# Layer 0's later modulation chunks as single VectorE steps, token-major products of 512 columns: a two-layer trunk on one Trainium2 core

## The chip, the cores and the metric

The kernel runs on one core of one Trainium2 chip. The metric is the time of an execution on the device in microseconds (us). The engines are named as in the profile: PE is TensorE (matmul), DVE is VectorE, ACT is ScalarE, POOL is GpSimd, SP is SyncE, which here issues the loads of the weights.

## What is computed

A trunk of two layers over 256 tokens of 1024 features (`x`) and 256 tokens of context (`xc`), which only the first layer updates.

```python
def layer_forward(x, xc, mod, mod_c, lp, update_ctx):
    sh1, sc1, g1, sh2, sc2, g2 = jnp.split(mod, N_MOD, axis=-1)      # 6 x 1024
    ...
    h = modulate(rmsnorm(x, lp['norm1_g']), sh1, sc1)
    p = h @ lp['w_in']                  # u, v, q, k, va, hyena, gates
    ...
    x = x + g1 * merge_branches(p, attn, lp)
    h = modulate(rmsnorm(x, lp['norm2_g']), sh2, sc2)
    x = x + g2 * conv_ffn(h, lp)
    # the same for xc, if update_ctx

def merge_branches(p, attn, lp):
    a = spatial_gating_mixer(...); hy = hyena_mixer(...)
    g_a, g_b, g_c = jnp.split(jax.nn.sigmoid(p[..., OFF_GATE:]), N_BRANCH, axis=-1)
    m = g_a * (a @ wb[0]) + g_b * (attn @ wb[1]) + g_c * (hy @ wb[2])
    return m @ lp['w_out']

    # for each layer i:
    mod = (jax.nn.silu(c) @ ada_w[i] + ada_b[i])[:, None, :]
    mod_c = (jax.nn.silu(c_ctx) @ ada_w[i] + ada_b[i])[None, None, :]
```

The modulation `mod` is thus a product of a vector (two vectors in layer 0, `c` and `c_ctx`) with a matrix of 1024 x 6144. Its first third (`sh1`, `sc1`) is needed at the layer's start, `g1` after the output projection, the rest in the feed-forward.

## The kernel before, in words

Activations lie feature-major: 128 features on the partitions, the tokens as columns, 512 in layer 0 (x and context) and 256 in layer 1. A dimension of 1024 is 8 tiles (`k`). Every product is done as three fp32r matmuls on parts split into high and low: `wh·rl`, `wh·rh`, `wl·rh` (`mm_k`, L308 to L310). The weights are loaded by SP into four slots of 128 x 2048 (`wraw`), their high part is cast by ACT (L248) and their low part subtracted by DVE (L255), both `AHEAD` parts before PE needs them; four parts are two pieces of 24 matmuls.

The work is a list `items` that `run_items` goes through: dense items (a chunk of weights and what to do with it), native items (a raw tile of weights that is used unsplit, loaded one ahead by `load_native`) and calls. Beside it runs `side`, a queue of generators (the filter of the hyena branch, the spatial gate, hyena, attention): `pump` lets them go on by a step at each evacuation in `fm_run`. A layer's items are in order: u and v; 6 hyena chunks; 4 chunks of q and k, 2 of va; 12 gate chunks, between them, two places later (`LEAD`), 12 branch products; the output projection; the feed-forward with 11 pairs of up-projections, in which the next layer's modulation is worked out too.

The products v and va are token-major (`tm_use`): the tokens are the stationary side, the weights the moving one, 256 columns at a time, in two chunks.

The modulation of layer 0: its first third comes at the start. Chunks 1 and 2 (features of index f = 16 to 47, in tiles of 128) are 16 native items `ada`, one behind each of the 6 hyena chunks, the 4 of q and k, the 2 of va and the first 4 gates. Each is 8 fp32 matmuls of 32 columns on four column tiles of PE (L379) and a `pump`; the eighth of a chunk is followed by a transpose on DVE (L422). Layer 1's modulation goes another way (`ada_f`, L401): a step on DVE multiplies a row of 128 x 1024 weights with `scb`, the SiLU of the vector spread over the partitions, and sums it into one column of `mod`; `spread_c` makes `scb` before the first of them.

What the names in the rows are: `hd`, `tot`, `nsum` and `Fe`/`Fo` belong to the hyena filter (`filters`), `P`, `yT`, `Zo` to the hyena convolution, `pc` to the short convolution behind the hyena chunks, `S`, `P__n` and `PT` to attention.

Of the kernel before, what the change touches and what calls it, by code (L numbers as in the profile page):

```python
# [19 lines left out]
D = 1024  # L20
KD = 8
# [73 lines left out]
def trunk_kernel(ctx: ExitStack, tc: tile.TileContext, A: dict, out: bass.AP):  # L95
# [110 lines left out]
    def cuts(kind, kt, ncols):  # L206


        if kind == "m":
            return [[(k, min(k + 4, kt), c, c + 128) for k in range(0, kt, 4)] for c in range(0, ncols, 128)]  # L210
        return [[(k, k + 2, 0, ncols) for k in range(0, kt, 2)]]

# [6 lines left out]
    def run_items():  # L219
# [49 lines left out]

        ctl.update(due=0, at=0, ahead=AHEAD[0], load=load_to, prime=prime)  # L270
        pos = 0
# [46 lines left out]
    def fm_run(tiles, R, s0, s1, mid=None):  # L318

        n = len(R[0])  # L320
        ps = [psm.tile([128, 512], F32, tag="m", name="mm") for _ in tiles]
        for k in range(n):
            mm_k([p[:, 0:s1 - s0] for p in ps], [W for W, _, _ in tiles], R, k, s0, s1, n)
        if mid:
            mid()
        for (_, evac, m), p in zip(tiles, ps):
            evacuate(evac(m, p, s0, s1))
            ctl["due"] += ctl["pace"][(s1 - s0) // 256 - 1 if n > 4 else 3]
            pump(int(ctl["due"]))
            ctl["due"] %= 1  # L330

    def fm_chunk(R, segs, evac, nm=2):
# [36 lines left out]

    def ada(l, ch, k):  # L370
        src = A["ada_w"][l, k * 128:(k + 1) * 128, ch * 2048:(ch + 1) * 2048]

        def use(w):
            if k == 0:
                ada.ps = psm.tile([128, 512], F32, tag="m", name="ada")
            ps = ada.ps
            v = w.rearrange("p (t j i) -> p j t i", j=4, i=32)
            for j in range(4):
                mm(ps[32 * j:32 * j + 32, :], lhsT=scc[:, k, :], rhs=v[:, j], start=(k == 0), stop=(k == KD - 1),  # L379
                   tile_position=(0, 32 * j))  # L380
            if k == KD - 1:
                ada_evac(l, ch, ps)
            pump()
        native(src, use)

    def spread_c():

        for m in range(2):
            act(out=scb[m], in_=scb[m], func=AF.Silu)  # L389

    def ada_f(l, ch, k, rows):


        def use(w):
            if ch == k == 0:
                spread_c()
            junk = U("junk", BF16, 1024)
            for t in range(2):
                for m in range(rows):
                    f = ch * 16 + 2 * k + t  # L400
                    vec.scalar_tensor_tensor(out=junk, in0=w[:, t * 1024:(t + 1) * 1024], scalar=1.0, in1=scb[m],  # L401
                                             op0=ALU.mult, op1=ALU.mult, accum_out=mod[l][:, f, m:m + 1])
            if k == KD - 1:
                t0 = ch * 16
                b = prm[:, P_AB + 48 * l + t0:P_AB + 48 * l + t0 + 16].unsqueeze(2).to_broadcast([128, 16, rows])
                o = mod[l][:, t0:t0 + 16, 0:rows]
                vec.tensor_tensor(out=o, in0=o, in1=b, op=ALU.add)
                gains(l, ch, rows)
        native(A["ada_t"][l - 1, ch * KD + k], use)

    def gains(l, ch, rows):

        if ch != 1:
# [3 lines left out]
            vec.scalar_tensor_tensor(out=gs[l][:, w_, :, 0:rows], in0=sc, scalar=1.0, in1=g, op0=ALU.add, op1=ALU.mult)  # L417

    def ada_evac(l, ch, ps):

        tr = U("adat")
        vec.transpose(out=tr, in_=ps)  # L422
        t0 = ch * 16
        b = prm[:, P_AB + 48 * l + t0:P_AB + 48 * l + t0 + 16].unsqueeze(2).to_broadcast([128, 16, 2])
        vec.tensor_tensor(out=mod[l][:, t0:t0 + 16, :], in0=tr.rearrange("p (t i) -> p t i", i=32)[:, :, 0:2], in1=b,
                          op=ALU.add)
        gains(l, ch, 2)

# [440 lines left out]
    def layer(l):  # L869
# [62 lines left out]

        def tm_use(c, ntt, dst, func, period=None):

            def use(piece):
                W = piece(0)
                rh, rl = S["H"]
                for t in range(ntt):
                    ps = psm.tile([128, 512], F32, tag="m", name="mt")
                    o = ps[:, 0:256]  # L940
                    for k in range(KD):
                        wh, wl = W[k]
                        x, y = rh[k][:, t * 128:(t + 1) * 128], rl[k][:, t * 128:(t + 1) * 128]
                        mm(o, lhsT=x, rhs=wl, start=(k == 0), stop=False)  # L944
                        mm(o, lhsT=x, rhs=wh, start=False, stop=False)  # L945
                        mm(o, lhsT=y, rhs=wh, start=False, stop=(k == KD - 1))  # L946
                    act(out=S[dst][t][:, c * 256:(c + 1) * 256], in_=o, func=func)  # L947
                    if (t + 1) % (period or ctl["pace"][2]) == 0:
                        pump()
            return use  # L950

        for c in range(2):
            dense(col(512 + c * 256), KD, 256, tm_use(c, 2 * nseg, "v", AF.Gelu, 1), "t")

        def go_sgu():
            S["sgu"] = start(sgu(l, nseg, S["u"], S["v"]))
            if l == 0:
                start(filters([iter(())], [(0, 1)]))
            S["part"] = []
        call(go_sgu)  # L960
# [24 lines left out]

        ada_todo = [(l, ch, k) for ch in (1, 2) for k in range(KD)] if l == 0 else []

        def hy_chunks():
            for c in range(6):
                dense(col(2560 + c * 256), KD, 256, late(lambda c=c: fm_chunk(S["H"], full, hy_evac(c))))  # L990
                if ada_todo:
                    ada(*ada_todo.pop(0))

            def go():
                S["hy"] = start(hyena(l, nseg, S["part"]))
            call(go)
# [8 lines left out]
        def qkv_chunks():  # L1005
            def alloc():
                S["qk"] = {(s, m): U("qk") for s in range(2) for m in range(4)}
                S["va"] = [U("va") for _ in range(4)]
            call(alloc, False)
            for i, c0, segs in ((0, 1024, full), (1, 1536, [(0, 512)])):  # L1010
                for c in range(2):
                    dense(col(c0 + c * 256), KD, 256,
                          late(lambda c=c, i=i, sg=segs: fm_chunk(S["H"], sg, qk_evac(i, c))))
                    if ada_todo:
                        ada(*ada_todo.pop(0))
# [6 lines left out]
            for c in range(2):  # L1022
                dense(col(2048 + c * 256), KD, 256, tm_use(c, 4, "va", AF.Copy), "t")
                if ada_todo:
                    ada(*ada_todo.pop(0))

# [44 lines left out]
        todo = [(b, j) for b in ORDER for j in range(4)]  # L1071
        for i in range(len(todo) + LEAD):
            if i >= LEAD and todo[i - LEAD][1] == 0:
                call(br_split(todo[i - LEAD][0]), False)
            if i < len(todo):
                b, j = todo[i]
                dense(col(4096 + b * 1024 + j * 256), KD, 256, late(lambda b=b, j=j: fm_chunk(S["H"], full, gate_evac(b, j))))
                if ada_todo:
                    ada(*ada_todo.pop(0))
            if i >= LEAD:  # L1080
# [3 lines left out]
                def before(b=b, j=j):  # L1084
                    if b == ORDER[-1]:
                        if j == 0:
                            S["M"] = [[], []]
                        for i in range(2):
                            S["M"][i] += fm("Mh" if i == 0 else "Ml", 2, T, F32R)
                call(before, False)  # L1090
                dense(wb[:, :, j * 256:(j + 1) * 256], 4, 256, late(lambda b=b, j=j: fm_chunk(S["B"], full, br_evac(b, j))))

# [5 lines left out]
        def res_evac(gate_t, j, nm, last):  # L1098
# [110 lines left out]

        for j in range(11):  # L1210
            up_pair(j)
            if j >= AJ:
# [139 lines left out]
    def finish():  # L1352
        rb = rbc.pop(0)
        for k in range(KD):
# [17 lines left out]

_NAMES = ["xT", "prm", "kst", "dec", "ada_w", "ada_0", "ada_t", "cc", "w_in", "sgu_w", "sgu_norm_g", "sgu_b", "rpb", "hy_filt_w3", "hy_skip",
          "w_branch", "w_out", "ffn_w_up", "ffn_w_down"]


def layout(i):
# [21 lines left out]
    for l in range(DEPTH):  # L1399
# [7 lines left out]
    r["ada_0"] = i["ada_w"][0, :, 0:2048].reshape(8, 128, 2, 4, 256).transpose(3, 0, 1, 2, 4).reshape(4, 8, 128, 512)  # L1407
    r["ada_w"] = i["ada_w"][0:1]

    r["ada_t"] = i["ada_w"][1:].transpose(0, 2, 1).reshape(DEPTH - 1, 24, 2, 128, D).transpose(0, 1, 3, 2, 4).reshape(  # L1410
        DEPTH - 1, 24, 128, 2 * D)
    r["cc"] = np.stack([i["c"][0], i["c_ctx"]])
# [36 lines left out]
```

## Time and profile before

| | us |
|---|---|
| median of 3 runs | 1455.67 (1454.6 to 1455.97) |
| the profiled execution | 1453.75 |
| its span in the profile | 1451.7 |
| PE busy | 1412.6 (97%) |
| DVE busy | 1006.3 (69%) |
| ACT busy | 666.9 (46%) |
| POOL busy | 89.2 (6%) |

The granted clock of PE is 0.995 on average. A matmul's duration overlaps with the next one's, so what a matmul costs is read from the distance of two starts, not from its duration. The span is what the profiler saw between first and last instruction, and the rows' times count from its start.

### The profile page before, as it was taken

What the parts mean: (1) busy time and instruction counts of PE and PEld (TensorE: products, weight loads), DVE (VectorE), ACT (ScalarE), POOL (GpSimd) and SP (SyncE); (2) the same over time, 40 slices, a digit from 0 to 9 for tenths busy, and PEclk for the clock granted to TensorE, in tenths of its full rate; (3) what the DMA queues carried; (4) which work ended last, traced back from release to release, by engine and by line L of the source; (5) the groups of instructions that cost most, each with busy time, mean ns of one, the idle gap of its engine ahead of it and who ended that gap; (6) DMA issues with size and microseconds to landing.
All of it is one profiled execution on the core that took longest, in us unless ns stands there. A gap on an engine that the chain in (4) does not pass through costs nothing.

```text
span 1451.7 us, 22050 instructions
## 1 busy us (share of the span) xinstructions
PE 1412.6 (97%) x8724; PEld 1215.9 (84%) x8724; DVE 1006.3 (69%) x1870; ACT 666.9 (46%) x1368; POOL 89.2 (6%) x96
## 2 busy tenths in 40 slices
PE   6999999999999999999999999999999999999997
PEld 4887777767787889988878778999789899999997
DVE  5666744676775567666887997578767787776575
ACT  4542332434664335533322433465336755665352
POOL 0020201110000000000001220000110000000000
PEclk9999999999999999999999999999999999999998
DMA  9835434233222523244488455545233445556542
GB/s 350 270 130 189 145 129 162 102 115 124 80 88 76 171 97 108 74 159 145 155 265 263 143 174 156 163 142 171 88 117 123 142 158 192 171 175 172 199 143 68
DMA packets 190594, 221.21 MB, mean 152 GB/s; under 512 B 5563, under 2 KB 174556, under 8 KB 185372
## 3 DMA queue, kind: packets, MB, share of 16 engines
q1 hardware_dynamic: 184848, 206.06, 43.0%
q0 software_dynamic: 3344, 10.75, 2.5%
q10 hardware_dynamic: 2300, 3.01, 0.7%
q8 instruction: 68, 1.11, 0.3%
q14 instruction: 34, 0.28, 0.1%
HBM read 216.65 MB, written 1.05 MB: 150 GB/s over the span
## 4 chain that ended last, share of the span: by engine, by line
PE 82%; DVE 9%; DMA 3%; ACT 3%; issue 1%; ACTq 0%; POOL 0%; SPq 0%; DVEq 0%; POOLq 0%
PE mm L308 22%; PE mm L310 22%; PE mm L309 22%; DMA w<-w_in 2%; DVE wp L255 2%; PE mt L944 1%; PE mt L945 1%; PE mt L946 1%; PE pv L813 1%; PE PT L800 1%; DMA aw<-ada 1%; PE S L776 1%; PE ada L379 1%; ACT wp L248 1%; PE Ze L634 1%
## 5 line engine op out<-in xcount | busy, mean ns | idle before, releaser
L308 PE MATMUL mm<-hl,wp 128*128 128x256 f32 (+1 forms) x1476 | 500.5, 339 | 0.8 <-DVE hl L479 0.7
L310 PE MATMUL mm<-hh,wp 128*128 128x256 f32 (+1 forms) x1476 | 491.5, 333 | 0.5 <-DVE wp L255 0.5
L309 PE MATMUL mm<-hh,wp 128*128 128x256 f32 (+1 forms) x1476 | 491.2, 333 | 0.0
L255 DVE TENSOR_TENSOR wp<-w,wp 128x512 fp32r<-128x512 f32 (+1 forms) x576 | 375.3, 695 | 24.3 <-ACT wp L248 21.2
L248 ACT CAST wp<-w 128x512 fp32r<-128x512 f32 (+1 forms) x576 | 321.4, 610 | 94.9 <-DMA w<-ffn_w_down 45.7
L308 PEld LDWEIGHTS mm<-hl,wp 128*128 128x128 f32 x1476 | 280.3, 190 | 37.4 <-issue 6.4
L309 PEld LDWEIGHTS mm<-hh,wp 128*128 128x128 f32 x1476 | 280.4, 190 | 29.4 <-issue 3.1
L310 PEld LDWEIGHTS mm<-hh,wp 128*128 128x128 f32 x1476 | 280.2, 190 | 28.4 <-DVE wp L255 0.7
L308 PE MATMUL mm<-ml,wp 128*128 128x256 f32 (+1 forms) x392 | 125.9, 321 | 0.0
L310 PE MATMUL mm<-mh,wp 128*128 128x256 f32 (+1 forms) x392 | 125.4, 320 | 0.0
L309 PE MATMUL mm<-mh,wp 128*128 128x256 f32 (+1 forms) x392 | 125.3, 320 | 0.0
L401 DVE SCALAR_TENSOR_TENSOR junk<-wn,scb 128x1024 bf16<-128x1024 f32 x64 | 79.2, 1238 | 2.8 <-ACT scb L389 1.4
L308 PEld LDWEIGHTS mm<-ml,wp 128*128 128x128 f32 x392 | 74.7, 190 | 6.0 <-issue 0.8
L309 PEld LDWEIGHTS mm<-mh,wp 128*128 128x128 f32 x392 | 74.7, 190 | 5.4
L310 PEld LDWEIGHTS mm<-mh,wp 128*128 128x128 f32 x392 | 74.7, 190 | 5.4
L1103 DVE SCALAR_TENSOR_TENSOR xT<-mm,mod,xT 128x256 f32<-128x256 f32 x72 | 33.7, 481 | 62.7 <-PE mm L310 61.1
L1137 ACT ACTIVATE a<-mm,prm 128x256 f32<-128x256 f32 (+1 forms) x48 | 30.8, 644 | 88.1 <-PE mm L310 87.0
L944 PE MATMUL mt<-wp,hh 128*128 128x256 f32 x224 | 64.3, 287 | 2.0 <-ACT va L947 1.3
L308 PE MATMUL mm<-bl,wp 128*128 128x512 f32 (+1 forms) x192 | 65.4, 341 | 0.0
L981 DVE SCALAR_TENSOR_TENSOR a<-mm,prm,a 128x255 f32<-128x255 f32 (+1 forms) x48 | 27.9, 582 | 53.2 <-ACT a L1137 53.2
L310 PE MATMUL mm<-bh,wp 128*128 128x512 f32 (+1 forms) x192 | 64.6, 336 | 0.0
L309 PE MATMUL mm<-bh,wp 128*128 128x512 f32 (+1 forms) x192 | 64.6, 336 | 0.0
(623 smaller groups left out, 2041.0 us busy)
## 6 DMA issues: line engine op xcount, KB each, us to landing
w<-w_in SPq DMA_DIRECT2D x56, 1024.0 KB, 5.2
w<-ffn_w_up SPq DMA_DIRECT2D x44, 1024.0 KB, 5.0
wn<-ada_t SPq DMA_DIRECT2D x24, 1024.0 KB, 5.0
wn<-ada_w SPq DMA_DIRECT2D x16, 1024.0 KB, 4.8
w<-w_branch SPq DMA_DIRECT2D x24, 512.0 KB, 3.4
w<-ffn_w_down SPq DMA_DIRECT2D x16, 768.0 KB, 5.1
w<-ffn_w_down SPq DMA_DIRECT2D x16, 640.0 KB, 4.5
aw<-ada SPq DMA_DIRECT2D x32, 256.0 KB, 5.4
```

The source lines that it names most:

```text
L248: nc.scalar.copy(h, src)
L255: vec.tensor_tensor(out=l_, in0=src, in1=spl[st["lo"]][0], op=ALU.subtract)
L308: mm(o, lhsT=wh, rhs=rl, start=(k == 0), stop=False)
L309: mm(o, lhsT=wh, rhs=rh, start=False, stop=False)
L310: mm(o, lhsT=wl, rhs=rh, start=False, stop=(k == n - 1))
L379: mm(ps[32 * j:32 * j + 32, :], lhsT=scc[:, k, :], rhs=v[:, j], start=(k == 0), stop=(k == KD - 1), tile_position=(0, 32 * j))
L401: vec.scalar_tensor_tensor(out=junk, in0=w[:, t * 1024:(t + 1) * 1024], scalar=1.0, in1=scb[m], op0=ALU.mult, op1=ALU.mult, accum_out=mod[ ...
L634: mm(pe, lhsT=fwd(2 * c), rhs=z[0], start=True, stop=True)
L944: mm(o, lhsT=x, rhs=wl, start=(k == 0), stop=False)
L981: vec.scalar_tensor_tensor(out=yv[:, :, 1:256], in0=pv[:, :, 0:255], scalar=w[:, 0:1], in1=yv[:, :, 1:256], op0=ALU.mult, op1=ALU.add)
L1103: vec.scalar_tensor_tensor(out=xs, in0=ps[:, s * 256 - s0:(s + 1) * 256 - s0], scalar=mod[l][:, gate_t + t, s:s + 1], in1=xs, op0=ALU.mult ...
L1137: act(out=y, in_=ps[:, 0:s1 - s0], func=AF.Identity, scale=w[:, 1:2], bias=b)
```

## The change

The 16 native items of layer 0 are gone from PE. In their place stand 64 steps on DVE (`ada_sum`): one for each f from 16 to 47 and each of the two vectors, with the operation that layer 1 uses. A generator (`ada_drip`) holds one weight tile as two half-rows, loads the half-row f + 2 when f is done, and is let on by `drip`, called at every evacuation of `fm_run` and for each token tile of `tm_use`. How many steps it makes each time is set along the list by `drops`: 2 in hyena chunks 0 to 2 (12 steps), 1 in hyena chunks 3 to 5 and in q and k (14), 0 in va, 1 in the gate chunks from the fifth on (16) and in the branch products from place 9 on (10), 0 in the output projection, and 1 from the third up-pair of the feed-forward on (the last 12). The bias and `gains` come for each 8 f. `spread_c` is called at the start of the spatial gate. The pumps that stood in the native items stay as calls. `ada_w` is no longer an input, and `ada_t` holds both layers.

Second, `tm_chunks` makes v and va (both layers) as 512 columns: two items of half the `k` each with 512 columns, four tiles of PSUM held between them, and one evacuation of 512 columns in the second.

```diff
-        return [[(k, k + 2, 0, ncols) for k in range(0, kt, 2)]]
+        n = 512 // ncols
+        return [[(k, k + n, 0, ncols) for k in range(0, kt, n)]]
...
             pump(int(ctl["due"]))
             ctl["due"] %= 1
+            drip()
...
-    def ada(l, ch, k):
...
-            for j in range(4):
-                mm(ps[32 * j:32 * j + 32, :], lhsT=scc[:, k, :], rhs=v[:, j], start=(k == 0), stop=(k == KD - 1),
-                   tile_position=(0, 32 * j))
-            if k == KD - 1:
-                ada_evac(l, ch, ps)
-            pump()
-        native(src, use)
...
+    def ada_sum(l, f, rows, w):
...
+        for m in range(rows):
+            vec.scalar_tensor_tensor(out=U("junk", BF16, 1024), in0=w, scalar=1.0, in1=scb[m], op0=ALU.mult,
+                                     op1=ALU.mult, accum_out=mod[l][:, f, m:m + 1])
+            yield
+        if f % 8 == 7:
...
+    def ada_drip():
...
+        w = wraw.tile([128, 2048], F32, tag="w", name="wn")
...
+        def load(f):
+            if f < 48:
+                h = (f % 2) * 1024
+                nc.sync.dma_start(out=w[:, h:h + 1024], in_=A["ada_t"][0, f // 2][:, h:h + 1024])
+        load(16)
+        load(17)
+        yield
+        for f in range(16, 48):
+            yield from ada_sum(0, f, 2, w[:, (f % 2) * 1024:(f % 2) * 1024 + 1024])
+            load(f + 2)
+        del w
+        ctl["native"]()
+
+    def drip():
+        for _ in range(ctl.get("drops", 0)):
+            if ctl["drip"] and not step(ctl["drip"]):
+                ctl["drip"] = None
...
+                    if h == 0:
+                        tiles.append(psm.tile([128, 512], F32, tag="m", name="mt"))
+                    for i, (wh, wl) in enumerate(W):
+                        k = 4 * h + i
...
-                    act(out=S[dst][t][:, c * 256:(c + 1) * 256], in_=o, func=func)
+                        mm(tiles[t], lhsT=x, rhs=wl, start=(k == 0), stop=False)
+                        mm(tiles[t], lhsT=x, rhs=wh, start=False, stop=False)
+                        mm(tiles[t], lhsT=y, rhs=wh, start=False, stop=(k == KD - 1))
+                    if h:
+                        act(out=S[dst][t], in_=tiles[t], func=func)
...
+        def tm_chunks(c0, ntt, dst, func, period=None):
+            tiles = []
+            for h in range(2):
+                dense(w_in[:, 4 * h:4 * h + 4, c0:c0 + 512], 4, 512, tm_use(h, ntt, dst, func, tiles, period), "t")
...
+                spread_c()
+                ctl["drip"] = ada_drip()
+                step(ctl["drip"])
...
+                if c % 3 == 0:
+                    drops(2 - c // 3)
...
+            drops(0)
+            tm_chunks(2048, 4, "va", AF.Copy)
...
+            drops(int(i >= 4))
...
+                drops(int(i >= 9))
...
+        drops(0)
...
+            if j == 2:
+                drops(1)
```

On DVE, in the hyena chunks of layer 0, this is the order before from the split of the filter's last weights (`w3l`) to the first `hd`:

```order
L175 TENSOR_TENSOR w3l<-w_1378,w3h 128x512
L175 TENSOR_TENSOR w3l<-w_1379,w3h 128x512
L255 TENSOR_TENSOR wp<-w,wp 128x512 x2
L981 SCALAR_TENSOR_TENSOR pc<-mm,prm,pc 128x2x255
L983 SCALAR_TENSOR_TENSOR pc<-mm,prm,pc 128x2x255
L550 TENSOR_TENSOR hd<-fh,dec 128x512 x2
```

and this after (L381 are the new steps):

```order
L381 SCALAR_TENSOR_TENSOR junk,mod_85<-wn,scb_83 128x1024
L175 TENSOR_TENSOR w3l<-w_1288,w3h 128x512
L175 TENSOR_TENSOR w3l<-w_1289,w3h 128x512
L256 TENSOR_TENSOR wp<-w,wp 128x512 x2
L991 SCALAR_TENSOR_TENSOR pc<-mm,prm,pc 128x2x255
L993 SCALAR_TENSOR_TENSOR pc<-mm,prm,pc 128x2x255
L551 TENSOR_TENSOR hd<-fh,dec 128x512 x2
L381 SCALAR_TENSOR_TENSOR junk,mod_85<-wn,scb_82 128x1024
```

The steps now stand between the filter's own instructions, the weights' subtracts and the short convolution. On PE, at the filter's spectrum, before:

```order
L583 MATMUL nrm<-tot,ones 128x512
L586 MATMUL Fe<-fe,kst 128x512
L587 MATMUL Fo<-fe,kst 128x512
L379 MATMUL ada<-wn,scc 32x512 x4
L586 MATMUL Fe<-fo,kst 128x512
L587 MATMUL Fo<-fo,kst 128x512
```

and after:

```order
L584 MATMUL nrm<-tot,ones 128x512
L587 MATMUL Fe<-fe,kst 128x512
L588 MATMUL Fo<-fe,kst 128x512
L587 MATMUL Fe<-fo,kst 128x512
L588 MATMUL Fo<-fo,kst 128x512
```

The `ada` matmuls between the side work's own are gone. On SP's queue, in the same chunks, before, with what each load waits for in brackets (L235 loads `w`, L268 a native tile):

```order
L235 DMA w<-w_in 128x8x256 [waits DMAHW0_49,DVE_49,Activation_49]
L268 DMA wn<-ada_w 128x2048 [waits DMAHW5_49,DMAHW2_49,PE_49]
L235 DMA w<-w_in 128x8x256 [waits DMAHW1_49,DVE_49,Activation_49]
L268 DMA wn<-ada_w 128x2048 [waits DMAHW3_49,PE_49]
L235 DMA w<-w_in 128x8x256 [waits DMAHW4_49,DVE_49,Activation_49]
```

and after (L407 loads a half-row):

```order
L236 DMA w<-w_in 128x8x256 [waits DMAHW7_49,DMAHW5_49,Activation_49]
L407 DMA wn<-ada_t 128x1024 [waits DMAHW2_49,DVE_49]
L407 DMA wn<-ada_t 128x1024 [waits DMAHW4_49,DVE_49]
L236 DMA w<-w_in 128x8x256 [waits DMAHW0_49,Activation_49]
L407 DMA wn<-ada_t 128x1024 [waits DMAHW6_49,DVE_49]
L407 DMA wn<-ada_t 128x1024 [waits DMAHW7_49,DVE_49]
L236 DMA w<-w_in 128x8x256 [waits DMAHW3_49,Activation_49]
```

The native tile waited for PE; the half-rows that take its place wait for DVE.

## Rows read from the trace of the kernel before

**Rows 1.** The page: span, then busy us, share and instructions of each engine.

```profile
span 1451.7 us, 22050 instructions
PE 1412.6 (97%) x8724; PEld 1215.9 (84%) x8724; DVE 1006.3 (69%) x1870; ACT 666.9 (46%) x1368; POOL 89.2 (6%) x96
```

**Rows 2.** Waits of PE: engine, line, releaser: us in total, times, longest.

```profile
PE PT L800 <- DVE P__3411 L789: 0.6, 1, 0.6
```

**Rows 3.** Timeline of PE around one `ada`: start us, us, engine, line, op.

```profile
109.94 0.39 PE L310 MATMUL mm<-hh,wp 128*128 128x512 f32 x1
...
111.59 0.39 PE L309 MATMUL mm<-hh,wp 128*128 128x512 f32 x1
```

**Rows 4.** Timeline of PE: two runs of equal matmuls, first and last.

```profile
52.56 0.39 PE L308 MATMUL mm<-hl,wp 128*128 128x512 f32 x1
...
55.05 0.39 PE L310 MATMUL mm<-hh,wp 128*128 128x512 f32 x1
...
57.00 0.28 PE L944 MATMUL mt<-wp,hh 128*128 128x256 f32 x1
...
60.84 0.28 PE L946 MATMUL mt<-wp,hl 128*128 128x256 f32 x1
```

**Rows 5.** Groups of L379 (duration ns, starts) and L944 (busy, mean ns | idle).

```profile
L379 PE MATMUL ada<-wn,scc x128: 592/605/617, 98.1 to 336.0; 128*32 128x512 f32 x128
...
L944 PE MATMUL mt<-wp,hh 128*128 128x256 f32 x224 | 64.3, 287 | 2.0 <-ACT va L947 1.3
```

**Rows 6.** Timeline of DVE: layer 1's modulation steps.

```profile
653.08 1.23 DVE L401 SCALAR_TENSOR_TENSOR junk<-wn,scb 128x1024 bf16<-128x1024 f32 x1
...
654.35 1.23 DVE L401 SCALAR_TENSOR_TENSOR junk<-wn,scb 128x1024 bf16<-128x1024 f32 x1
```

**Rows 7.** Waits of DVE from 91 to 152.2, and its timeline at 91.9.

```profile
DVE pc L981 <- ACT pc L973: 20.9, 10, 3.1
DVE ss L703 <- ACT ss L702: 2.5, 1, 2.5
...
91.93 0.75 DVE L981 SCALAR_TENSOR_TENSOR pc<-mm,prm,pc 128x510 f32<-128x510 f32 x1 [1.14 <-ACT pc L973]
```

**Rows 8.** Timeline of DVE, POOL and PE: the filter's sum.

```profile
153.46 1.28 DVE L550 TENSOR_TENSOR hd<-fh,dec 128x512 f32<-128x512 f32 x2
...
154.74 4.67 POOL L560 TENSOR_TENSOR tot<-tot,abs 128x512 f32<-128x512 f32 x3
...
159.47 1.05 PE L573 MATMUL nsum<-ones,tot 128*128 128x2 f32 x8 [0.74 <-POOL tot L560]
```

**Rows 9.** Timeline of DVE and PE: two places of the hyena convolution.

```profile
265.85 0.69 DVE L657 TENSOR_TENSOR P<-yr 128x512 f32<-128x512 f32 x1
...
266.60 0.49 PE L681 MATMUL yT<-kst,P 128*128 128x128 f32 x2
...
325.24 0.46 PE L681 MATMUL yT<-kst,P 128*128 128x128 f32 x2 [1.51 <-DVE P L657]
```

**Rows 10.** Windows: from:to, us, busy of PE, PEld, DVE, ACT, POOL (count), clock, DMA.

```profile
340.00:460.00 120.00, 118.34 (x613) 93.61 (x612) 85.10 (x186) 75.45 (x181) 4.80 (x6) 1.00 0.27 88
660.00:700.00 40.00, 40.00 (x178) 33.13 (x177) 26.91 (x42) 15.31 (x26) 0.00 (x0) 1.00 0.41 142
```

**Rows 11.** Timeline of ACT: the gap near 86 to 91, and the SiLU of `scb`.

```profile
91.12 0.78 ACT L973 ACTIVATE pc<-mm,prm 128x512 f32<-128x512 f32 x1 [4.76 <-PE mm L310]
...
607.89 2.01 ACT L389 ACTIVATE scb<-scb 128x1024 f32<-128x1024 f32 x2
```

**Rows 12.** One weight load, its cast, and the page's loads: KB, us to landing.

```profile
97.37 0.38 SPq L235 DMA_DIRECT2D w<-w_in  x1
...
105.60 1.13 ACT L248 CAST wp<-w 128x512 fp32r<-128x512 f32 x2
...
w<-w_in SPq DMA_DIRECT2D x56, 1024.0 KB, 5.2
...
w<-w_branch SPq DMA_DIRECT2D x24, 512.0 KB, 3.4
```

More of the change, by code (lines that the diff above doesn't have):

```diff
@@ L268, in load_native @@
                 nc.sync.dma_start(out=raw[i], in_=items[i][1])
-        ctl.update(due=0, at=0, ahead=AHEAD[0], load=load_to, prime=prime)
+        ctl.update(due=0, at=0, ahead=AHEAD[0], load=load_to, prime=prime, native=load_native)
         pos = 0
@@ L368, in silu_c @@
         act(out=scc[:, :, 0:2], in_=prm[:, P_CC:P_CC + 16].rearrange("p (k m) -> p k m", m=2), func=AF.Silu)
-    def ada(l, ch, k):
[L371 to L377, printed above, removed]
-            for j in range(4):
-                mm(ps[32 * j:32 * j + 32, :], lhsT=scc[:, k, :], rhs=v[:, j], start=(k == 0), stop=(k == KD - 1),
-                   tile_position=(0, 32 * j))
-            if k == KD - 1:
-                ada_evac(l, ch, ps)
-            pump()
-        native(src, use)
     def spread_c():
@@ L389, in spread_c @@
             act(out=scb[m], in_=scb[m], func=AF.Silu)
+    def ada_sum(l, f, rows, w):
[4 more added lines that the diff above has]
+        if f % 8 == 7:
+            t0 = f - 7
+            b = prm[:, P_AB + 48 * l + t0:P_AB + 48 * l + t0 + 8].unsqueeze(2).to_broadcast([128, 8, rows])
+            o = mod[l][:, t0:t0 + 8, 0:rows]
+            vec.tensor_tensor(out=o, in0=o, in1=b, op=ALU.add)
+            if t0 in (8, 32):
+                gains(l, t0 // 16, rows)
     def ada_f(l, ch, k, rows):
         def use(w):
-            if ch == k == 0:
-                spread_c()
-            junk = U("junk", BF16, 1024)
             for t in range(2):
[L399 to L409, printed above, removed]
+                for _ in ada_sum(l, ch * 16 + 2 * k + t, rows, w[:, t * 1024:(t + 1) * 1024]):
+                    pass
+        native(A["ada_t"][l, ch * KD + k], use)
+    def ada_drip():
[16 more added lines that the diff above has]
+                ctl["drip"] = None
     def gains(l, ch, rows):
@@ L417, in gains @@
             vec.scalar_tensor_tensor(out=gs[l][:, w_, :, 0:rows], in0=sc, scalar=1.0, in1=g, op0=ALU.add, op1=ALU.mult)
[L419 to L427, printed above, removed]
     sq_acc, diag, rbc = {}, {}, {}
@@ L931, in layer, with tm_use @@
                 dense(col(c * 256), KD, 256, late(lambda c=c: fm_edge(S["H"], halves, u_evac(c), 2, st1, 4, NH1[1])))
-        def tm_use(c, ntt, dst, func, period=None):
+        def tm_use(h, ntt, dst, func, tiles, period):
             def use(piece):
@@ L938, in use @@
                 for t in range(ntt):
[L939 to L942, printed above, removed]
+                    if h == 0:
+                        tiles.append(psm.tile([128, 512], F32, tag="m", name="mt"))
+                    for i, (wh, wl) in enumerate(W):
+                        k = 4 * h + i
                         x, y = rh[k][:, t * 128:(t + 1) * 128], rl[k][:, t * 128:(t + 1) * 128]
-                        mm(o, lhsT=x, rhs=wl, start=(k == 0), stop=False)
-                        mm(o, lhsT=x, rhs=wh, start=False, stop=False)
-                        mm(o, lhsT=y, rhs=wh, start=False, stop=(k == KD - 1))
-                    act(out=S[dst][t][:, c * 256:(c + 1) * 256], in_=o, func=func)
+                        mm(tiles[t], lhsT=x, rhs=wl, start=(k == 0), stop=False)
[3 more added lines that the diff above has]
+                        act(out=S[dst][t], in_=tiles[t], func=func)
                     if (t + 1) % (period or ctl["pace"][2]) == 0:
                         pump()
+                    drip()
             return use
-        for c in range(2):
-            dense(col(512 + c * 256), KD, 256, tm_use(c, 2 * nseg, "v", AF.Gelu, 1), "t")
+        def tm_chunks(c0, ntt, dst, func, period=None):
+            tiles = []
+            for h in range(2):
+                dense(w_in[:, 4 * h:4 * h + 4, c0:c0 + 512], 4, 512, tm_use(h, ntt, dst, func, tiles, period), "t")
+        tm_chunks(512, 2 * nseg, "v", AF.Gelu, 1)
         def go_sgu():
@@ L984, in conv_sides, with drops @@
                                      op0=ALU.mult, op1=ALU.add)
-        ada_todo = [(l, ch, k) for ch in (1, 2) for k in range(KD)] if l == 0 else []
+        extra = [1] * 16 if l == 0 else []
+        def drops(n):
+            if l == 0:
+                call(lambda: ctl.update(drops=n), False)
         def hy_chunks():
             for c in range(6):
+                if c % 3 == 0:
+                    drops(2 - c // 3)
                 dense(col(2560 + c * 256), KD, 256, late(lambda c=c: fm_chunk(S["H"], full, hy_evac(c))))
-                if ada_todo:
-                    ada(*ada_todo.pop(0))
+                if extra:
+                    extra.pop()
+                    call(pump, False)
             def go():
@@ L1013, in qkv_chunks @@
                           late(lambda c=c, i=i, sg=segs: fm_chunk(S["H"], sg, qk_evac(i, c))))
-                    if ada_todo:
-                        ada(*ada_todo.pop(0))
+                    if extra:
+                        extra.pop()
+                        call(pump, False)
             def go():
@@ L1021, in qkv_chunks @@
             call(go)
[L1022 to L1025, printed above, removed]
+            drops(0)
+            tm_chunks(2048, 4, "va", AF.Copy)
+            for _ in range(2):
+                if extra:
+                    extra.pop()
+                    call(pump, False)
         hy_chunks()
@@ L1077, in layer @@
                 dense(col(4096 + b * 1024 + j * 256), KD, 256, late(lambda b=b, j=j: fm_chunk(S["H"], full, gate_evac(b, j))))
-                if ada_todo:
-                    ada(*ada_todo.pop(0))
+                if extra:
+                    extra.pop()
+                    call(pump, False)
             if i >= LEAD:
@@ L1371 @@
 HYY = (1, 1)
-_NAMES = ["xT", "prm", "kst", "dec", "ada_w", "ada_0", "ada_t", "cc", "w_in", "sgu_w", "sgu_norm_g", "sgu_b", "rpb", "hy_filt_w3", "hy_skip",
+_NAMES = ["xT", "prm", "kst", "dec", "ada_0", "ada_t", "cc", "w_in", "sgu_w", "sgu_norm_g", "sgu_b", "rpb", "hy_filt_w3", "hy_skip",
           "w_branch", "w_out", "ffn_w_up", "ffn_w_down"]
@@ L1407, in layout @@
     r["ada_0"] = i["ada_w"][0, :, 0:2048].reshape(8, 128, 2, 4, 256).transpose(3, 0, 1, 2, 4).reshape(4, 8, 128, 512)
-    r["ada_w"] = i["ada_w"][0:1]
-    r["ada_t"] = i["ada_w"][1:].transpose(0, 2, 1).reshape(DEPTH - 1, 24, 2, 128, D).transpose(0, 1, 3, 2, 4).reshape(
-        DEPTH - 1, 24, 128, 2 * D)
+    r["ada_t"] = i["ada_w"].transpose(0, 2, 1).reshape(DEPTH, 24, 2, 128, D).transpose(0, 1, 3, 2, 4).reshape(
+        DEPTH, 24, 128, 2 * D)
     r["cc"] = np.stack([i["c"][0], i["c_ctx"]])
```

## The prediction

> **What bounds the kernel now.** I read the busy shares first, then what TensorE (PE) waits for, and only then the places that the change touches, one by one. PE is busy 1412.6 of 1451.7 us and VectorE (DVE) 1006.3 [rows 1]. The waits of PE in the parts that the change touches are short: those that I use are 0.6 to 1.5 us [rows 2, 5, 8, 9]. So the kernel is a line of matmuls: what leaves PE is gained, and what comes to DVE costs only where PE has to wait for DVE's order. The forecast is therefore a sum over PE's line, and the costs are looked for place by place.
>
> **What leaves PE: the modulation.** A block `ada` is 8 matmuls. Around one, the product's matmuls start at 109.94, then (two after it) 111.59 [rows 3]. Without it they would follow each other at 0.2264 us, which is (55.05 − 52.56)/11 [rows 4], so the second would have started at 110.39. The block costs 111.59 − 110.39 = 1.20 us. There are 128 such matmuls, all in layer 0 [rows 5], so 16 blocks: 16 × 1.20 = 19.2 us.
>
> **What leaves PE: the short matmuls.** The 256-column products of v and va start every (60.84 − 57.00)/32 = 0.120 us, the 512-column ones every 0.2264 us [rows 4]. One of 512 in place of two of 256 saves 0.0136 us. Each of the three lines has 224 (one of them in [rows 5]), so 672 become 336: 336 × 0.0136 = 4.6 us. A rule speaks against this term: the Trainium skill, page "TensorE: Matmul & The Clock Gate", section "Wait — 56ns, not 53.3ns?", gives warm back-to-back matmuls N columns at 2.4 GHz plus about 2.5 ns each. By it halving the count would save an estimated 336 × 2.5 ns = 0.8 us and the forecast would be some 4 us later. The rows differ from it: 120 ns against 106.7 for 256 columns and 226.4 against 213.3 for 512, so about 13 ns for each matmul with its own weight load; the measurement decides.
>
> Together 19.2 + 4.6 = 23.8 us can be gained.
>
> **What comes to DVE.** The added operation stands in the trace already, for layer 1: one row-step is 1.23 us and the next starts 1.26 us after it (653.08 and 654.35) [rows 6]. 64 × 1.26 = 81 us. DVE has 1451.7 − 1006.3 = 445 us idle [rows 1], so the average hides it; four places may not. The two transposes that go and the split of bias and gains into groups of 8 cancel within a microsecond on a DVE that has room.
>
> (1) The filter of the hyena branch. By the instruction order 15 steps (18.9 us) come between 91 and the `hd` of 153.46 [rows 8]. In that stretch DVE waits 20.9 + 2.5 us, nearly all for the evacuations of ScalarE (ACT) [rows 7]. Of this 1.1 us lies ahead of the first step [rows 7], and four of the removed blocks (4.8 us) shorten the stretch, so 20.9 + 2.5 − 1.1 − 4.8 = 17.5 us of room for 18.9 us. The room is in ten pieces of at most 3.1 us, so it won't be filled fully; I take DVE to be 2 us late at `hd`. In before, POOL adds up `tot` from 154.74 for 4.67 us, and PE waited 0.74 us for that at `nsum` [rows 8]. With five blocks gone PE would be there at 159.47 − 0.74 − 6.0 = 152.7; `tot`, started behind the `hd`, is ready at 159.41 − 4.8 + 2 = 156.6. The wait is 3.9 us where it was 0.74: **3.2 us lost**. With no lag it is 1.2, with a lag of 6 us 7.2.
>
> (2) Two blocks that filled a wait. At 325.24 PE waits 1.51 us for `P` of DVE [rows 9]; the last block ahead of it, between the `Zo` of the same chain and this `yT`, held PE and not DVE, so its 1.2 us turn into wait. At 266.60 `yT` starts just behind `P`, which was ready at 265.85 + 0.69 = 266.54 [rows 9]: the gain of the block ahead of it is lost too. **2.4 us lost.**
>
> (3) Attention. From 340 to 460 us PE is busy 118.34 and DVE 85.10 of 120 [rows 10]. Of the 26 steps at the gates from the fifth and the branch products from the tenth place on, 11 stand in the order between score blocks (13.9 us). DVE's 35 us of idle hold them, but a score block's `P` scaling can come just behind a step. Where this is tight already, PE waits 0.5 to 0.6 us (three such waits, one shown in [rows 2]); there I take a full step each: **3 × 1.26 = 3.8 us lost**. Bounds: 0, if the step always falls into the gaps, and 13.9, if all 11 delay PE.
>
> (4) Elsewhere: 8 steps in the q and k chunks, the last gates and branches, and 12 steps in the feed-forward. There DVE is idle 13 of 40 us with layer 1's steps running [rows 10] and PE is busy all 40. I take 0; if the twelve all delayed PE it would be 15.1.
>
> ACT gets the two SiLU of `scb` at the layer's start, not in the feed-forward: 2.01 us [rows 11] and the load of a table. ACT was idle 4.76 us before its evacuation of 91.12 [rows 11], and that hides them; without that cover they would cost those 2 us and the load once. The evacuations of the token-major products go from two of 256 columns to one of 512 but come all in the second half. PE waited 1.3 us for one of them [rows 5]; that wait can go or double, ±1.3, taken as 0.
>
> **Sum.** 23.8 − 3.2 − 2.4 − 3.8 = 14.4 us. The durations come from the profiled execution, which took 1453.75 us, 2.05 more than its span. That is 1453.75 − 14.4 = 1439.35; the median of the runs shown is 1.9 us above the profiled execution, so on its basis **1441 us**.
>
> **Rivals.**
> - *All is hidden.* The steps fall into DVE's gaps and `hd` isn't late; only what (2) takes and part of the rest is lost or not even that: 1455.7 − 23.8 = 1432. For it: 445 us of idle, and PE's waits are already tiny. Against it: the filter's place, where 18.9 us meet 17.5.
> - *DVE is the bound in two stretches.* The upper bounds of (1) and (3): 7.2 + 2.4 + 13.9 = 23.5 against 23.8, so 1455. For it: attention's chain of score, softmax and scaling goes through DVE for each block, and its share there is 71%. Against it: the idle there is more than twice what is added.
> - *Late weights; this one makes it slower.* SyncE's queue (SP) now holds, between the loads of `w`, half-row loads that wait for DVE to be done with the step before the last; a load of `w` behind them is late with them. A lag of two steps (2.52 us) and the transfer of a half row in between (5.2 − 3.4 = 1.8 us for 512 KB more) make 4.3 us [rows 6, 12]. The cover: a load issued at 97.37 has landed at 102.6 and its cast starts at 105.60 [rows 12], 3.0 us later. The remaining 1.3 us would come at each of the 29 weight loads that have such rows ahead (6 hyena, 4 q and k, 8 gates, 5 branches, 6 feed-forward): 38 us against 23.8, so 1470. It decides from 23.8/29 = 0.82 us each. For it: the order shows these waits on DVE, and SP works them one after the other. Against it: PE needs the parts of that cast only two pieces (2 × 24 × 0.2264 = 10.9 us) later, so the cover is really about 14 us, and in before SP already waited for DVE's subtract of the weights.
> - *It doesn't do what it says.* No `ada` step of layer 0's later chunks is left on PE in the order, and the token-major rows are of 512 columns; it could only be that 512 columns cost as much as two of 256. Then 4.6 us are missing: 1445.5, inside the forecast's range.
>
> **How the numbers follow.** Forecast 0.62, with its own range 1436 to 1448: the losses of (1) between 1.2 and 7.2, of (3) between 0 and some 7, the 1.3 of `va` either way. All hidden 0.15, DVE the bound 0.12, late weights 0.08, and not as it says 0.03. What a measurement here can tell from no change is 0.2%, 2.9 us either way: 1452.8 to 1458.6. DVE the bound ends half inside that. So faster 0.85, same 0.06, slower 0.09. The range must leave out no more than 2 in 10: 1431 takes in all but the rounding of "all is hidden", and 1452 takes in the better half of the second rival.
>
> **What would show it.** After the change there should be no `ada` on PE between 98 and 336, PE busy some 20 us less, DVE some 80 more. `nsum` should wait about 4 us for POOL and `yT` near 310 about 2.7 for DVE; waits for `P` in attention should be fewer than ten and about 1 us each. The pitch of the token-major matmuls should be 0.226. Wrong would be: a row of waits for the casts of weights behind DMAs (late weights), waits for DVE summing to over 20 us in attention, or a DVE that is behind through the whole hyena stretch, seen as `hd` more than 5 us late against the matmuls.

## The result, and the profile after

The changed kernel takes 1465.53 us (median of 4 runs, 1462.05 to 1469.48), the kernel before 1455.76 in the same comparison: a ratio of 1.0075 with the interval 1.0059 to 1.0091. It is slower by some 10 us. The forecast was 1441, the range 1431 to 1452.

The page of the changed kernel, in the columns of [rows 1]. The profiled execution took 1469.48 us.

```profile
span 1467.4 us, 21273 instructions
PE 1405.3 (96%) x8260; PEld 1206.5 (82%) x8260; DVE 1072.1 (73%) x2001; ACT 662.6 (45%) x1353; POOL 91.3 (6%) x96
```

PE has 464 matmuls less (16 blocks of 8 and 336 of the token-major ones) and DVE is busy 66 us more. PE was idle 39 us before and is idle 62 us now. To see where, I take the start of the same instruction in several traces and list the stretches between them, in us (worked out from the traces; e1, e2 and e12 are experiments, below). Each stretch begins where the one above it ends. The profiled execution of the changed kernel is the slowest of its four runs, so the table explains 15.7 us (1451.7 against 1467.4), more than the 9.8 between the medians.

| stretch | before | after | e1 | e2 | e12 |
|---|---|---|---|---|---|
| start to the first hyena evacuation `pc` | 91.1 | 89.1 | 89.4 | 90.9 | 89.3 |
| to attention's first exponential | 250.3 | 237.5 | 237.0 | 250.8 | 238.3 |
| to the output projection's first `xT` | 185.6 | 191.0 | 191.0 | 185.6 | 186.8 |
| to the feed-forward's first activation | 46.1 | 47.7 | 47.6 | 46.2 | 46.1 |
| to the last `xT` of its first down half | 219.8 | 241.7 | 220.5 | 244.0 | 219.9 |
| to the first `xT` of its second down half | 108.4 | 111.2 | 108.6 | 110.9 | 108.6 |
| to the last `fin` of the kernel | 547.1 | 546.1 | 543.7 | 545.1 | 545.2 |

Up to attention the changed kernel is 14.8 us ahead (2.0 + 12.8). It loses 5.3 by the output projection, 1.5 across it, and 21.9 + 2.8 in the feed-forward of layer 0.

Two views show the large loss. Windows of 700 to 800 us, in the columns of [rows 10], first after, then before:

```profile
700.00:800.00 100.00, 88.49 (x374) 69.95 (x372) 59.82 (x113) 21.22 (x38) 7.46 (x14) 0.98 0.59 194
```

```profile
700.00:800.00 100.00, 100.00 (x440) 81.68 (x439) 80.45 (x147) 28.19 (x50) 7.43 (x14) 1.00 0.76 242
```

PE, DVE and ACT do less here after the change, and the DMA too: nothing is at its limit, so something waits in a ring. PE itself, which from 700 to 900 us waited only 0.3 us before, waits for what comes late from the others (line, releaser: us in total, times, longest):

```profile
PE fh L548 <- DVE hs L175: 4.9, 1, 4.9
PE mm L311 <- DVE wp L256: 3.6, 3, 2.0
PE nrm L584 <- DVE tot L579: 3.4, 2, 2.3
PE fps L497 <- ACT fs L508: 3.4, 1, 3.4
PE mm L309 <- ACT wp L249: 1.0, 1, 1.0
```

Waits of SP's queue from 700 to 800, in the same columns, after and before:

```profile
SPq L236 <- DVE junk L381: 57.1, 7, 9.3
SPq L236 <- DVE mod L388: 17.8, 2, 9.1
SPq L269 <- DVE wp L256: 13.7, 9, 4.7
```

```profile
SPq L268 <- DVE junk L401: 65.7, 10, 8.3
SPq L235 <- DVE wp L255: 30.3, 12, 12.5
SPq L268 <- DVE mod L407: 12.2, 2, 6.7
```

The partners have been exchanged. Before, a weight load (L235) waits for the weights' own split (`wp`), and a native tile of layer 1 (L268) for modulation steps (`junk`). After, the weight load (L236) waits for modulation steps. One turn of this ring, in SP's, DVE's and ACT's timelines of after:

```profile
678.25 6.75 SPq L269 DMA_DIRECT2D wn<-ada_t  x2
...
779.90 0.38 SPq L236 DMA_DIRECT2D w<-ffn_w_down  x1
781.11 0.33 SPq L269 DMA_DIRECT2D wn<-ada_t  x1
788.17 1.22 DVE L381 SCALAR_TENSOR_TENSOR junk<-wn,scb 128x1024 bf16<-128x1024 f32 x1
789.31 1.22 DVE L381 SCALAR_TENSOR_TENSOR junk<-wn,scb 128x1024 bf16<-128x1024 f32 x1
790.57 0.38 SPq L236 DMA_DIRECT2D w<-ffn_w_up  x1
...
798.61 1.66 ACT L249 CAST wp<-w 128x512 fp32r<-128x512 f32 x3 [10.50 <-DMA w<-ffn_w_up]
```

The weight load starts at 790.57, right behind the two steps, its cast 8 us later; the steps themselves stand behind the evacuation of an item that waited for the load before. So loads follow each other at 10.67 us. Before, with chunks of `ffn_w_down`, they followed at 6.57 us:

```profile
742.35 0.37 SPq L235 DMA_DIRECT2D w<-ffn_w_down  x1
...
748.92 0.37 SPq L235 DMA_DIRECT2D w<-ffn_w_down  x1
```

The row at 678.25 is how it begins: two native tiles in a row. Layer 1's natives start with the second up-pair (`next_ada` in `up_pair`), and each use loads the next one. The drip ends only in the up-pairs behind, and its last line loads the next one early (`ctl["native"]`). From there on two native tiles are ahead. The addresses in the two programs show what this does to the four slots (in the order of the loads; w is weights, n a native tile, the number its slot):

```
before: n0 w2 n1 w3 n0 w2 n1 w3 n0 w2 ...
after:  n1 w2 n0 w3 n2 w1 n3 w0 n1 w2 n0 w3 n2 w1 ...
```

Before, weights and natives keep two slots each. After, each weight load follows a native tile in its slot.

The second loss is at the output projection. DVE's timeline in the last branch products after, and PE's wait behind it:

```profile
506.30 1.22 DVE L381 SCALAR_TENSOR_TENSOR junk<-wn,scb 128x1024 bf16<-128x1024 f32 x1
507.44 0.69 DVE L1088 SCALAR_TENSOR_TENSOR Ml<-m,Mh 128x512 fp32r<-128x512 f32 x1
508.04 0.68 DVE L256 TENSOR_TENSOR wp<-w,wp 128x512 fp32r<-128x512 f32 x1
508.64 0.68 DVE L1080 SCALAR_TENSOR_TENSOR gt<-gt,mm 128x512 f32<-128x512 f32 x1
509.36 0.69 DVE L1081 TENSOR_TENSOR m<-m,gt 128x512 f32<-128x512 f32 x1
509.97 1.22 DVE L381 SCALAR_TENSOR_TENSOR junk<-wn,scb 128x1024 bf16<-128x1024 f32 x1
...
515.53 0.50 PE L309 MATMUL mm<-Ml,wp 128*128 128x512 f32 x1 [2.71 <-DVE Ml L1088]
```

DVE works without a gap and needs 3.67 us for each evacuation; PE needs 12 × 0.2264 = 2.72 us for the matmuls of one. Without the step (1.14 us, from 506.30 to 507.44) DVE needs 2.53 us and keeps up.

Other waits of PE after the change, in the columns of [rows 2]:

```profile
PE yT L682 <- ACT wp L249: 4.5, 2, 2.7
PE yT L682 <- DVE P L658: 2.3, 1, 2.3
PE nsum L574 <- POOL tot L561: 1.9, 1, 1.9
```

Of the 4.5 us in the first line, 1.8 lie in layer 1 and stand in the trace of before too.

### The profile page after: what moved, and what is told of

Same layout as the page of the kernel before. It is cut to its first block, busy times and chain, and to the rows that moved or that the text cites. A ratio compares the mean times of both kernels' runs of the same rounds, so it can differ in the third digit from the quotient of the medians.

```text
span 1467.4 us, 21273 instructions
## 1 busy us (share of the span) xinstructions
PE 1405.3 (96%) x8260; PEld 1206.5 (82%) x8260; DVE 1072.1 (73%) x2001; ACT 662.6 (45%) x1353; POOL 91.3 (6%) x96
## 4 chain that ended last, share of the span: by engine, by line
PE 71%; DVE 13%; DMA 7%; issue 4%; ACT 4%; POOL 1%; SPq 0%; ACTq 0%; DVEq 0%; POOLq 0%
PE mm L309 19%; PE mm L310 19%; PE mm L311 19%; DVE junk L381 3%; DMA w<-ffn_w_down 3%; DMA aw<-ada 2%; DVE wp L256 2%; PE mt L945 2%; PE mt L947 2%; PE mt L946 2%; DMA w<-ffn_w_up 1%; ACT wp L249 1%; PE pv L814 1%; PE PT L801 1%; PE S L777 1%
## 5 line engine op out<-in xcount | busy, mean ns | idle before, releaser
L381 DVE SCALAR_TENSOR_TENSOR junk<-wn,scb 128x1024 bf16<-128x1024 f32 x128 | 156.5, 1251 | 0.1
L439 ACT ACTIVATE sqt<-xT 128x256 f32<-128x256 f32 x48 | 20.0, 417 | 81.1 <-DVE xT L1127 80.9
```

Of the source, the lines that this page charges most:

```text
L381: vec.scalar_tensor_tensor(out=U("junk", BF16, 1024), in0=w, scalar=1.0, in1=scb[m], op0=ALU.mult, op1=ALU.mult, accum_out=mod[l][:, f, m: ...
```

## The experiments

There was no run e3: the 512 columns alone, on the kernel before, weren't tried, because four PSUM tiles held over both halves and the tile that a block `ada` sums in are five, and the pool has four.

**e1: one native tile ahead.**

```diff
         del w
-        ctl["native"]()
```

> The changed kernel, but the generator of the modulation steps no longer loads a native tile when it ends, so that layer 1's modulation is loaded one tile ahead, as in the kernel before, and not two. Theory 'slots': the second native tile turned the rotation of the four weight slots, so each load of feed-forward weights waits for two modulation steps; without it the 23 us that the trace after shows lost between 720 and 790 us come back: 1465.5 - 23 = 1442 us (1438 to 1448). Rival 'VectorE': the loss there is the added VectorE time (12 steps in the up-projections and what they push back), and the order of the loads is a symptom: no change, 1462 to 1469 us.

1443.9 us (1442.07 to 1447.12), ratio 0.9929 (0.991 to 0.9947). 21.6 us come back, and the stretches of the feed-forward are within 0.7 us of those of before (220.5 and 108.6 in the table). The loads have their partners again, in SP's waits from 700 to 800:

```profile
SPq L269 <- DVE junk L381: 50.1, 8, 8.2
SPq L236 <- DVE wp L256: 28.1, 11, 12.6
SPq L269 <- DVE mod L388: 20.0, 3, 7.8
```

All DVE steps are still there (DVE is busy 1072.0 us, the changed kernel 1072.1): the rival falls.

**e2: the kernel before with two native tiles ahead.**

```diff
-        ctl.update(due=0, at=0, ahead=AHEAD[0], load=load_to, prime=prime)
+        ctl.update(due=0, at=0, ahead=AHEAD[0], load=load_to, prime=prime, native=load_native)
...
             up_pair(j)
+            if j == 4 and l == 0:
+                call(lambda: ctl["native"](), False)
```

> The kernel before with one edit: after the fifth up-pair of layer 0 one more native tile of layer 1's modulation is loaded, so that from there on two are ahead. No step, no matmul and no column count changes. Theory 'slots': weights then take the slots of native tiles and the feed-forward loses about what the changed kernel lost there, 15 to 23 us: 1471 to 1479 us. Rival 'VectorE': within 0.2% of before, 1453 to 1459 us.

1482.54 us (1478.84 to 1486.02), ratio 1.0189 (1.0168 to 1.021): 27 us slower, a little more than expected, by one load made early and nothing else. The loss stands in the same two stretches, 24.2 and 2.5 us, and the slots run in the same turn as in the changed kernel. SP's waits from 700 to 800:

```profile
SPq L235 <- DVE junk L401: 64.8, 8, 9.4
SPq L268 <- DVE wp L255: 15.5, 9, 4.7
```

**e10: five slots.**

```diff
-    wraw = ctx.enter_context(tc.tile_pool(name="wraw", bufs=RAWB + 1))
+    wraw = ctx.enter_context(tc.tile_pool(name="wraw", bufs=RAWB + 2))
...
-NU = 76
+NU = 72
```

> The changed kernel with five weight slots in place of four (and 72 activation buffers of 2 KB in place of 76, which pays for the slot). The generator still loads its extra native tile, so two are ahead as in the changed kernel, but in the order of the loads the weights now keep two slots to themselves and the native tiles rotate over the other three. If what costs is that weights wait for a native tile's slot, the 21.6 us come back: 1444 us (1440 to 1448). If two native tiles ahead cost by themselves (their transfers, or a place of theirs in SP's queue): 1460 to 1468 us.

1449.54 us (1447.01 to 1452.69), ratio 0.9964 (0.9954 to 0.9974): above the expected range, and far below the other. With two natives ahead still, the stretch to the first down half's last `xT` is 219.9 us where the changed kernel has 241.7: the ring is gone. That the total is 5.6 us above e1 lies mostly in the stretch to attention's first exponential, 243.2 us against 237.0; there a `yT` waits 4.95 us for DVE (at 259.09) in place of 2.31. That the four buffers less do this is likely and was not tried by itself. So it is the slot, not the second tile.

**e4 and e5: the last branch products without steps**, on the changed kernel and on e1; the 8 steps in the va products instead.

```diff
-            drops(0)
+            drops(1)
             tm_chunks(2048, 4, "va", AF.Copy)
...
-                drops(int(i >= 9))
+                drops(int(i == 9))
```

> The changed kernel, with the 8 steps taken out of the last four branch products and made in the va products instead (one for each token tile). Theory 'tail': in the last branch products VectorE needs 3.7 us for each evacuation of 2.7 us of matmuls, and the output projection waited 5.5 us for it (against the trace before); moved, 4 to 6 us come back at the output projection, and if the feed-forward's loss stays as it is 1460 us (1457 to 1464). Rival: the feed-forward's loads set the pace behind it and swallow the gain: 1463 to 1469 us; or the va products' 8 steps cost as much there.

> Both edits: one native tile ahead and no steps in the last four branch products. Theories 'slots' and 'tail' together: 1465.5 - 23 - 5 = 1437 us (1434 to 1443), with no wait for Ml above 1 us and weight loads that wait for the split of weights and not for modulation steps. Rival 'VectorE': 1460 us or more.

e4: 1468.12 us (1466.61 to 1469.93), ratio 1.0091 (1.0076 to 1.0106). e5: 1444.14 us (1442.54 to 1446.27), ratio 0.9926 (0.9912 to 0.9941). Neither is faster than its parent, and yet the tail was right: from attention's first exponential to the first `xT` e5 takes 186.8 us, e1 191.0. The same steps cost as much in their new place. PE's timeline in e5:

```profile
261.06 0.80 PE L681 MATMUL yT<-kst,P 128*128 128x128 f32 x2 [9.08 <-DVE P L657]
```

In e1 this wait is 2.31 us: in the va products the hyena convolution's chain on DVE is what PE waits for next, and 6.9 us go there by the stretches (243.9 against 237.0).

**e6: e1 with 256 columns** (the token-major products as before).

> The kernel of e1 (one native tile ahead) with the token-major products as before: 256 columns, 672 matmuls. By the prediction's pitch (0.0136 us for each of 336 pairs) this is 4.6 us slower than e1, 1448.5 us; by what the trace of e1 shows over the four products (7.9 us less from their first to their last matmul, waits at their edges included) up to 1452 us; if 512 columns brought nothing, 1444.

1447.38 us (1446.37 to 1450.1), ratio 0.9958 (0.9941 to 0.9975). By the medians 3.5 us slower than e1 where the pitch gives 4.6; the runs of both (1442.07 to 1447.12 and 1446.37 to 1450.1) lie too far apart to settle the size. The traces say more: from their first to their last matmul the four products take 81.5 us in e1 and 86.1 in e6, which is the 4.6. And the `yT` behind va waits 2.31 us in e1 (at 252.73) and 1.21 in e6 (at 254.13): 1.1 us of the gain goes into a wait for DVE.

**e7: short steps**, on e1.

```diff
+        n = 32 if l == 0 else 1024
...
-            vec.scalar_tensor_tensor(out=U("junk", BF16, 1024), in0=w, scalar=1.0, in1=scb[m], op0=ALU.mult,
+            vec.scalar_tensor_tensor(out=U("junk", BF16, 1024)[:, 0:n], in0=w[:, 0:n], scalar=1.0, in1=scb[m][:, 0:n], op0=ALU.mult,
```

> The kernel of e1, with layer 0's 64 steps over 32 of the 1024 columns, so that their sums are not the modulation: the loads, the waits and the order stay, some 74 us of VectorE work go. What it is faster than e1 by is the whole price of the steps on VectorE. By the trace of e1 that is at least the 5.5 us at the output projection and 1.5 in attention, with the hyena places up to 12: 1432 to 1437 us, which would also be what the change could bring at best. If VectorE's time isn't what costs (but the loads or the order), 1442 to 1445 us.

1437.14 us (1434.75 to 1440.13), ratio 0.9886 (0.9866 to 0.9906): 6.8 us faster than e1. That is the whole price of some 64 us of DVE work (busy 1072.0 us in e1, 1008.3 here). The two profiled executions lie somewhat further apart (spans of 1441.0 and 1432.9 us); by the starts in them 1.6 us come in the hyena chunks, 1.1 in attention, 5.5 in the last branch products and 0.9 in the feed-forward. The 1.6 us are no wait for DVE: from the first `pc` to `nsum` both take 63.4 us, and behind it e1 has a stretch at half clock (last section) that this trace lacks. The waits of `yT` (4.5 and 2.3) and `nsum` (1.9) are in this trace too, to the tenth: the steps don't make them.

**e8: the last 8 steps at the output projection**, on e1 (`drops(int(i == 9))` at the branches, `drops(1)` at the projection and `drops(0)` behind it).

> The kernel of e1, with the 8 steps of the last four branch products made at the 8 evacuations of the output projection. There VectorE has room (two additions of 0.48 us and a weight subtract of 0.6 us for 5.4 us of matmuls), so the 5.5 us that the last branch products lost come back: 1438 us (1436 to 1441), with no wait for Ml above 1 us. Rival: the steps hold up the norm behind the output projection by as much: 1443 to 1446.

1449.06 us (1446.84 to 1452.54), ratio 0.9965 (0.9949 to 0.9982), 5.2 us slower than e1: the rival held, and by more than it said. The wait for `Ml` is gone, but the norm behind the projection is late: from the first `xT` to the first activation it takes 55.1 us, e1 47.6. PE's waits from 500 to 600 us in e8:

```profile
PE mm L309 <- DVE hl L479: 3.8, 4, 1.8
PE ssum L452 <- ACT sqt L438: 2.6, 1, 2.6
```

**e9: steps out of the q and k products**, on e8, into the branch products 5 to 8 (`drops(0)` and `drops(int(5 <= i <= 9))`).

> The kernel of e8, with the 8 steps at the q and k products made at the branch products 5 to 8 instead, in attention. In e1 the trace shows yT waiting 2.3 us for VectorE at 252.7, behind the q and k products; if their steps put VectorE behind, up to 2.3 us come back there, and attention loses about 0.06 us for each step (it lost 1.5 us for its steps so far): 1436 us. If attention is the tighter place, 1438 to 1446 us.

1455.46 us (1451.73 to 1459.5), ratio 1.0009 (0.9996 to 1.0022), 6.4 us slower than e8. `yT` still waits 2.3 us, and from attention's first exponential to the first `xT` it takes 191.2 us where e8 takes 186.8: attention bore 11 steps among its score blocks for 1.1 us, and 8 more cost 4.4. The profiled executions lie further apart than the medians (spans of 1457.4 and 1447.5 us); 3.4 us of that come in layer 1, where no step differs and where this trace has two stretches at half clock that e8 lacks, at 1066 and 1138.

**e11 and e12: the last branch products' steps in the hyena chunks 3 to 5 (`drops(2)` in all six; two of the eight fall to the feed-forward), or at the first four gates (`drops(1)` there)**, on e1.

> The kernel of e1, with steps taken out of the last four branch products: six of them are made in the hyena chunks 3 to 5 (two for each evacuation there too), the rest in the feed-forward. The tail gives back 5.5 us. In the hyena chunks the 18 steps so far cost 1.6 us by the trace of e7 against e1; if VectorE still has room there: 1439 us (1437 to 1442). If it is full there (the filter's place has 17.5 us of room by the prediction, and 15 steps fill it): 1442 to 1448.

> The kernel of e1, with the 8 steps of the last four branch products made at the first four gate products, beside the end of the hyena convolution. The tail gives back 5.5 us. If VectorE's chain of the convolution has room: 1439 us. As the 8 steps at va cost 6.6 us in that neighbourhood, and its yT wait for VectorE: 1444 to 1448 us, which I hold more likely.

e11: 1444.06 us (1443.28 to 1445.32), ratio 0.9927 (0.9912 to 0.9942), as e1: the hyena chunks lose what the tail gives back (`nsum` waits 2.5 us for POOL, `fh` 1.8 for DVE). e12: 1440.2 us (1439.36 to 1442.34), ratio 0.9905 (0.9888 to 0.9921). It is faster than the kernel before, the changed one and, by a little, e1, and 3.1 us above the short steps. I had held that less likely: by the stretches only 1.3 us are lost up to attention. By the starts the steps beside the end of the convolution cost 2.6 us there, and 1.3 come back because this trace has no stretch at half clock behind `nsum`, where e1 has one.

## Why the prediction was wrong

The sum held as far as it went, in part by luck. Its terms give 14.4 us; without the early native load (e1) the kernel is 11.5 us faster than before, and with the tail's steps at the gates (e12) 14.9. What failed is point (4), "Elsewhere ... I take 0", in two places.

The feed-forward: I counted the drip's steps and its half-row loads, and not the native tile that its last line loads. Layer 1's natives have begun with the second up-pair, and this one is a second ahead. The prediction nowhere works out which load follows which in the four slots. It cost 21.6 us (e1), or 27 in a kernel with nothing else changed (e2).

The last branch products: DVE's idle time was averaged over attention, and over 660 to 700 us, and "the last gates and branches" hidden by it. There DVE needs 2.53 us of 2.72, and a step of 1.14 more can't be hidden: 5.5 us.

By its own steps:

- The blocks, 19.2 us, and the short matmuls, 4.6: both right. Behind each block that is gone the matmuls of the changed kernel start 1.22 us further ahead of before (from 2.0 to 8.1 us over the five blocks between 95 and 156), where I took 1.20. For the matmuls, e6 against e1 gives 4.6 in the products themselves and 3.5 in the medians. The rule of 2.5 ns for each (the Trainium skill, page "TensorE: Matmul & The Clock Gate", section "Wait — 56ns, not 53.3ns?") would have given an estimated 0.8 us; the traces bear out the rows.
- The steps on DVE, 81 us: two that follow each other start 1.14 us apart (788.17 and 789.31), not 1.26, and DVE is busy 66 us more.
- The filter, 3.2: `nsum` waits 1.9 us where it waited 0.74 [rows 8], 1.2 more, which is the prediction's own figure for no lag. It does so with short steps too, so DVE was not late at `hd`, and what I gave for the lag was not there. In the trace after, some 1.7 us come on top by PE's clock (below). That the two together come near 3.2 is luck.
- The two filled waits, 2.4: `yT` waits 2.31 us for `P` where [rows 9] show no wait; with 256 columns (e6) it is 1.21, the block's 1.2, and the rest goes with the 512 columns. The second waits 2.69 where it waited 1.51, 1.2 more as I took it. The row names ACT's cast for this wait, but `P`, which `yT` reads, was ready only 0.04 us before the cast was, so "about 2.7 for DVE" came true:

```profile
309.22 0.69 DVE L658 TENSOR_TENSOR P<-yr 128x512 f32<-128x512 f32 x1
309.33 0.62 ACT L249 CAST wp<-w 128x512 fp32r<-128x512 f32 x1 [0.58 <-DVE m L1078]
```

- Attention, 3.8: some 1.1 by the starts before and after and by e7. The waits for `P` grew in number from 3 to 5 and stayed at 0.3 to 0.6 us; a full step each was too much.
- Of the rivals "late weights" had the direction, and the mechanism by half: weights did come late because SP's loads waited for DVE, and its sign, a cast that waits for a DMA, is the row at 798.61. But it placed them at the 29 loads with half rows ahead, where no product waited for its weights, and priced them by a lag in the queue. It was the slot, and it came after the last half row (678.25; PE's first wait for weights in the feed-forward is at 748.91).

## What to carry to other kernels

Where tiles of two kinds share a pool, work out which load follows which in a slot, and not only how many slots there are: one more tile ahead cost 27 us here. A prefetch at the end of a moved task is an instruction of that task, to be checked against what has begun by then. And idle time hides a step only if it lies between the same two evacuations: 3.67 us of work against 2.72 of matmuls is a loss even on an engine that is idle 27% of the time.

## What the runs showed of the hardware

A wait of PE can cost more than its length. In e1 PE waits 1.90 us at 152.79, and from 154.5 on the granted clock is half, 1.2 GHz; timeline of PE, and the window (columns of [rows 10]):

```profile
152.79 0.27 PE L573 MATMUL nsum<-ones,tot 128*128 128x2 f32 x1 [1.90 <-POOL tot L560]
...
155.70 0.63 PE L309 MATMUL mm<-hl,wp 128*128 128x512 f32 x1
156.13 0.63 PE L310 MATMUL mm<-hh,wp 128*128 128x512 f32 x1
...
158.59 0.39 PE L311 MATMUL mm<-hh,wp 128*128 128x512 f32 x1
158.81 0.39 PE L309 MATMUL mm<-hl,wp 128*128 128x512 f32 x1
```

```profile
154.50:157.90 3.40, 3.40 (x10) 2.66 (x9) 3.37 (x6) 0.00 (x0) 0.14 (x1) 0.51 0.36 104
```

Matmuls of 512 columns come at 0.43 us and then at 0.23 again. Eight of them at the lower level cost 8 × (0.43 − 0.226) = 1.6 us, nearly as much as the wait. But the same wait was followed by no fall in e7 (rows below, in the same columns), nor in e4 and e12, so its length alone doesn't decide:

```profile
153.43 0.27 PE L574 MATMUL nsum<-ones,tot 128*128 128x2 f32 x1 [1.90 <-POOL tot L561]
```

```profile
154.50:157.90 3.40, 3.40 (x16) 2.79 (x17) 3.33 (x9) 0.00 (x0) 0.78 (x1) 1.00 0.49 130
```

The wait of 0.74 us in [rows 8] was followed by none either. What decides is open, and so one trace can show 1.6 us more or less than another at a place where nothing else differs. Before its last 15 us the trace of before has two stretches at half clock and that of the changed kernel ten, two of them longer, which goes with the mean clock of 0.995 and 0.984.
